# Dense expert blocks written ahead of the last two top-k, and the gate tables' one-hots as contiguous pair blocks

## The chip, the cores and the metric

The kernel runs on one core of one Trainium2 chip. The metric is device time in microseconds (us) of one execution. The engines are named as in the profile: PE is TensorE (matmul; PEld is its weight load, which overlaps), DVE is VectorE, ACT is ScalarE, POOL is GpSimd, SP is SyncE, whose queue issues most of the DMA transfers. PEclk is the TensorE clock that was granted, as a share of full speed.

## The reference

One layer of a decoder is computed for 1056 tokens (1024 prompt, 32 sample), width 1024. It is a mixer (RWKV-7 and pooling, not touched here), then a layer of 16384 single-neuron experts, then an input gate and norms. The change lies in the expert layer:

```
q = (xb @ wq).reshape(128, 8, 2, 128)                  # 8 heads, two halves of the key
s1, s2 = q[:, :, 0] . sub_keys[0], q[:, :, 1] . sub_keys[1]     # 128 scores each
v1, i1 = lax.top_k(s1, 16);  v2, i2 = lax.top_k(s2, 16)
cand = v1[..., :, None] + v2[..., None, :]             # 256 candidates
sc, ci = lax.top_k(cand, 16)
expert = e1 * 128 + e2                                 # e1, e2: i1, i2 at the winners
gate = softmax(sc)
act = gelu(u_tab[expert] . xb) * gate                  # 8 * 16 experts a token
out = sum(act * v_tab[expert])
```

## The kernel before, in words

The program is a list of instructions that a list scheduler has ordered for each engine; where two instructions are ready at once, the one that was written first goes first. Each engine then runs its own list strictly in order. SBUF memory comes from pools that stand on a left and a right stack. A pool that is opened where another was closed takes its memory, and the first writer of a tile waits for the last reader of what lay there.

**Ahead of the experts.** Projections, the RWKV scan in chunks, then for each group of tokens the output projection and the scores. `phase_c` puts the scores of a tile of 128 tokens into DRAM (`scs`, copied by ACT at L750, to `sc_d`), and `top` reads them back in four quarters (`scq`, two buffers, by SP's queue at L759).

**Top-k.** `top` and `select` run for each tile of 128 tokens, nearly all on DVE (L762 to L852, some 120 instructions a tile) with short steps on ACT (copies, the exponential at L830) and POOL (`code`, and half of the `oh` steps at L848).

**Two ways through the experts.** Of the 1056 tokens 672 take the *dense* way, in which all 16384 experts are computed for them as matmuls and multiplied by a table of gates that is zero nearly everywhere. The other 384, three tiles of 128, take the *gather* way: for every token its 8 x 16 rows of `u` and of `v` are fetched by indirect DMAs.

**Gate tables (dense way).** The end of `select` makes them from two one-hots. For four tokens at a time, a tile `ab` holds three blocks of 128 x 4: the one-hot of e1, the one-hot of e2 times the high part of the gate, and times the low part. L875 (DVE) compares an iota with e1 and e2 in one operation of 1024 elements, L877 (DVE) and L878 (POOL; DVE in every third) multiply 512 elements each, and eight matmuls of 128x128 (L881) make the table of four tokens in PSUM. ACT copies it out (L882). `e16` holds e1, e2 and the gates' two parts, each as 128 tokens in a row. There are 168 such steps, from 771 to 1377 us of the span, interleaved with the projections and scores of the later groups.

**Dense blocks.** There are 128 expert blocks of 128. `ublock(b)` loads a block of uT (`eraw`, three buffers, SP's queue, L1060), splits it in a high and a low part (`ehi` on ACT at L1062, `elo` on DVE at L1064, two buffers each), runs 48 matmuls of 336 columns (L1086) and a gelu on ACT (L1092). `ugate(b)` multiplies by the gates (DVE L1148) and splits the product into `wh` (ACT L1150) and `wl` (DVE L1152) in pool `dw`. After each eight blocks (VG = 8) come eight `vblock`s, which load and split a block of vP in the same manner and run 48 matmuls each over the eight `wh`/`wl`. "U8" and "V03" below are ublock 8 and the vblock of group 0, column block 3. The first eight ublocks are run early (`upre`), into tiles `OT0` to `OT7`.

**Order around the change.** The pools `ws`, `mv`, `wc`, `tk` (top-k) stand on one stack of pools, `phases`. Three calls of `top` for the gather tiles come last in it; then `phases` is closed, `dw` and the gather's `rows` are opened on the memory that was freed, and the loop over the dense blocks begins. After it in the text, thus behind it in rank, stand the gather tiles: per row POOL issues an indirect DMA (L1189), DVE does one operation of 1024 elements (L1197 for `u`, L1206 for `v`). Each tile ends with eight transposes on PE (L1216). The layer's last part (`Tail`, input gate and norms, L1234 and on) ends the program.

Of the kernel before, what the change touches and what calls it, by code (L numbers as in the profile page):

```python
# [20 lines left out]
KB = D // 128  # L21
# [40 lines left out]
def body(ctx, tc, io):  # L62
    nc = tc.nc
    mm = nc.tensor.matmul
# [19 lines left out]
    def v3(ap, n):  # L84
        return ap.rearrange("p (a b) -> p a b", b=n)
# [667 lines left out]
    def top(tk, pos, m):  # L753
        V12 = tk.tile([128, HEADS, 2, TOPK], F32, name="V12", bufs=1)
        I12 = tk.tile([128, HEADS, 2, TOPK], U32, name="I12", bufs=1)
        for i in range(16):
            if i % 4 == 0:
                sq = tk.tile([128, 4, 128], F32, name="scq", bufs=2)
                nc.sync.dma_start(sq[:m], sc_d[TIDX[pos], :m, i:i + 4, :])  # L759
            s_ = sq[:m, i % 4, :]  # L760
            v8, i8 = V12[:m, i // 2, i % 2, :], I12[:m, i // 2, i % 2, :]
            nc.vector.max(v8[:, 0:8], s_)  # L762
            nc.vector.max_index(i8[:, 0:8], v8[:, 0:8], s_)  # L763
            s2 = tk.tile([128, 128], F32, name="s2", bufs=2)
            nc.vector.match_replace(s2[:m], v8[:, 0:8], s_, -BIG)  # L765
            nc.vector.max(v8[:, 8:16], s2[:m])
            nc.vector.max_index(i8[:, 8:16], v8[:, 8:16], s2[:m])  # L767
            yield
        yield from select(tk, pos, m, V12, I12)


    def select(tk, col, m, V12, I12):
# [87 lines left out]
        ps = PS("b3")  # L860
        for i in range(3):
            src = e12[:m, i, :] if i < 2 else gl[:m].rearrange("p a b -> p (a b)")
            nc.tensor.transpose(ps[:, i * 128:i * 128 + m], src, ident[:m, :m])
        e16 = gp.tile([128, 4, 128], F16, name="e16")
        pe = v3(ps, 128)
        ACT(e16[:, 0:2, :m], pe[:, 0:2, :m], AF.Copy)
        ACT(e16[:, 2, :m], pe[:, 2, :m], AF.Copy, scale=GS)
        STT(e16[:, 3, :m], pe[:, 2, :m], GS, e16[:, 2, :m], op0=ALU.mult, op1=ALU.subtract)
        for t1 in range(0, m, TC):
            st = gp.tile([128, EB, TC], F32, name="gst", bufs=2)  # L870
            for t2 in range(0, TC, 4):
                ps = PS("b3")
                t = t1 + t2
                ab = gp.tile([128, 3, EB, 4], F16, name="ab", bufs=3)
                TT(ab[:, 0:2], iota16[:, None, :, :].to_broadcast([128, 2, EB, 4]),  # L875
                   e16[:, 0:2, None, t:t + 4].to_broadcast([128, 2, EB, 4]), op=ALU.is_equal)
                TT(ab[:, 2], ab[:, 1], e16[:, 2, None, t:t + 4].to_broadcast([128, EB, 4]), op=ALU.mult)  # L877
                GLO(t)(ab[:, 1], ab[:, 1], e16[:, 3, None, t:t + 4].to_broadcast([128, EB, 4]), op=ALU.mult)  # L878
                for i in range(4):
                    for k in (2, 1):  # L880
                        mm(ps[:, i * 128:(i + 1) * 128], ab[:, k, :, i], ab[:, 0, :, i], start=k == 2, stop=k == 1)  # L881
# [147 lines left out]
                pass  # L1029


    ws = phases.enter_context(tc.tile_pool(name="ws", bufs=2))
    mv = phases.enter_context(tc.tile_pool(name="mv", bufs=1))
    work = phases.enter_context(tc.tile_pool(name="wc", bufs=1))
    tk = phases.enter_context(tc.tile_pool(name="tk", bufs=1))
    gstack = ExitStack()
    gp = gstack.enter_context(tc.tile_pool(name="gp", bufs=1))
    iota16 = gp.tile([128, EB, 4], F16, name="iota16")
    it = gp.tile([128, EB, TC], F32, name="gst", bufs=2)[:, :, 0:4]
    nc.gpsimd.iota(it, pattern=[[1, EB], [0, 4]], base=0, channel_multiplier=0, allow_small_or_imprecise_dtypes=True)  # L1040
# [9 lines left out]
    NWT = 3  # L1050
    DP = ((0, NH), (NH, NH))
    U = {}
    LOW = 0

    def PD():
        return dps.tile([128, 2, 512], F32, name="pd")
# [43 lines left out]
    for step in range(1, NG + 1):  # L1100
# [16 lines left out]
        if step == NG - 1:  # L1117
# [6 lines left out]
                nc.sync.dma_start(XH[:, k, :].bitcast(F32), xh_d[:, k, :])  # L1124
                nc.sync.dma_start(XL[:, k, :].bitcast(F32), xl_d[:, k, :])
            xs = [(XH[:, k, :], XL[:, k, :]) for k in range(KB)]
    for col in range(0, GT, 128):
        with tc.high_priority(offset=LOW if col else 0):
            for _ in top(tk, GB + col, min(128, GT - col)):
                pass  # L1130
    phases.close()

    NROW = 7
    dw = ctx.enter_context(tc.tile_pool(name="dw", bufs=1, reuse_waits="tile"))
    rstack = ExitStack()
    rows = rstack.enter_context(tc.tile_pool(name="rows", bufs=1, reuse_waits="tile"))
    dpt = ctx.enter_context(tc.tile_pool(name="dpt", bufs=2, space=bass.MemoryType.PSUM, reuse_waits="tile"))


    Ws, gqs = {}, {}  # L1140

    def ugate(b):
        if b % GQ == 0:
            gqs[0] = gqp.tile([128, NTC, GQ, TC], F32, name="gq")
            nc.sync.dma_start(gqs[0], g_d[b // GQ])
        wt_ = U[b]
        w3 = wt_.rearrange("p (c t) -> p c t", t=TC)
        TT(w3, w3, gqs[0][:, :, b % GQ, :], op=ALU.mult)  # L1148
        wh = dw.tile([128, ND], F32R, name="wh", bufs=VG + 1)
        ACT(wh, wt_, AF.Copy)  # L1150
        wl = dw.tile([128, ND], F32R, name="wl", bufs=VG + 1)
        TT(wl, wt_, wh.bitcast(F32), op=ALU.subtract)  # L1152
        Ws[b] = (wh, wl)

    def vblock(g, db):
        w = esplit(io["vP"][g, db])
        ps = PD()
        emm(ps, w, [Ws[b] for b in range(g * VG, (g + 1) * VG)], DP)
        if g:
            TT(halves(OT[db]), ps[:, :, :NH], halves(OT[db]), op=ALU.add)  # L1160
        else:
            ACT(halves(OT[db]), ps[:, :, :NH], AF.Copy)
        if g == EB // VG // 2:
            ht = wt_tile()
            nc.sync.dma_start(ht, hT_d[:, db, GA:GB])
            TT(OT[db], OT[db], ht, op=ALU.add)

    for g in range(EB // VG + 1):
        for b in range(g * VG, min((g + 1) * VG, EB)):
            if b not in U:  # L1170
                ublock(b)
            ugate(b)
            if b == g * VG and g:
# [216 lines left out]
```

## Time and profile before

| | |
|---|---|
| median of 3 runs | 3432.76 us (3430.71 to 3433.68) |
| profiled execution | 3432.96 us |
| its span | 3431.3 us |
| PE busy | 3233.8 us, 94% of the span |
| DVE busy | 2675.9 us, 78% |
| POOL busy | 1788.5 us, 52% |
| ACT busy | 1190.1 us, 35% |

The profiled execution is 0.2 us above the median, and 1.7 us of it lie outside the span. One slice of the page's 40 is 85.8 us. From about 1480 us to the end the dense blocks' matmuls run nearly without a gap. In front of them, from 771 to 1377 us, DVE is busy 573.3 of 606 us and PE 560.1. Between the two stages PE stands still once, for 59.7 us.

### The profile page before, as it was taken

The numbers are of one execution on the slowest core, as the hardware profiler recorded it, in microseconds if no ns is written. First come the engines' busy times: TensorE is split into PE (matmuls) and PEld (weight loads), VectorE is DVE, ScalarE is ACT, GpSimd is POOL, SyncE is SP. The second block draws the span as 40 slices with busy tenths as digits, with TensorE's granted clock in tenths as the row PEclk, the third lists the DMA queues.
The fourth block names the chain that finished last, engine by engine and source line by source line (L and its number), as shares of the span: only waits on it lengthen the run. The fifth ranks groups of instructions, "written<-read, shape, count | busy, mean of one in ns | idle before, by whom it ended". The sixth has DMA issues, their size and how long they took to land.

```text
span 3431.3 us, 57620 instructions
## 1 busy us (share of the span) xinstructions
PE 3233.8 (94%) x21831; PEld 3142.4 (92%) x21831; DVE 2675.9 (78%) x5365; ACT 1190.1 (35%) x1776; POOL 1788.5 (52%) x1434
## 2 busy tenths in 40 slices
PE   8997998999999899489999999999999999999997
PEld 7876988999989888489999999999999999999997
DVE  6777333269999889788888888888888888888656
ACT  6452523345555555222212222222222122222343
POOL 5434334235465365256666666665566666666225
PEclk9997999999999999789999999999999999999999
DMA  4567645768767877459999999998989999999524
GB/s 167 206 210 193 176 132 139 217 180 229 195 194 217 267 233 226 168 207 341 335 326 342 334 342 326 340 346 314 342 329 335 329 337 348 326 330 339 173 81 130
DMA packets 467861, 883.61 MB, mean 258 GB/s; under 512 B 129280, under 2 KB 252416, under 8 KB 463104
## 3 DMA queue, kind: packets, MB, share of 16 engines
q1 hardware_dynamic: 356992, 477.24, 43.3%
q0 software_dynamic: 110592, 402.70, 32.0%
q8 instruction: 171, 2.80, 0.3%
q14 instruction: 106, 0.87, 0.1%
HBM read 759.22 MB, written 120.60 MB: 256 GB/s over the span
## 4 chain that ended last, share of the span: by engine, by line
PE 71%; DVE 15%; DMA 4%; POOL 2%; issue 1%; ACT 1%; SPq 0%; DVEq 0%; ACTq 0%; POOLq 0%
PE pd L1086 56%; DVE ab L875 2%; PE ps L881 2%; PE ps L661 2%; PE ps L663 2%; PE ps L662 2%; DVE ab L877 1%; PE ps L526 1%; DMA sraw<-wq 1%; PE ps L521 1%; DVE oh L847 1%; DVE h L718 1%; DVE I L763 1%; DVE s L765 1%; DVE I L767 1%
## 5 line engine op out<-in xcount | busy, mean ns | idle before, releaser
L1189 POOL DMA_INDIRECT row<-v,idx x384 | 533.2, 1389 | 322.8 <-DVE po L1206 147.4
L1189 POOL DMA_INDIRECT row<-u,idx x384 | 538.1, 1401 | 298.8 <-DVE row L1197 119.1
L1062 ACT ACTIVATE ehi<-eraw 128x1024 fp32r<-128x1024 f32 x278 | 294.8, 1060 | 1140.4 <-PE pd L1086 1088.6
L1086 PE MATMUL pd<-wh,ehi 128*128 128x336 f32 (+1 forms) x2112 | 507.1, 319 | 66.2 <-ACT wh L1150 59.7
L1086 PE MATMUL pd<-XH,elo 128*128 128x336 f32 x2176 | 515.5, 318 | 4.5 <-POOL elo L124 2.8
L1086 PE MATMUL pd<-XL,ehi 128*128 128x336 f32 x2176 | 514.8, 317 | 0.0
L1086 PE MATMUL pd<-XH,ehi 128*128 128x336 f32 x2176 | 512.7, 316 | 0.0
L1086 PE MATMUL pd<-wl,ehi 128*128 128x336 f32 (+1 forms) x2112 | 506.9, 319 | 0.7 <-DVE wl L1152 0.7
L1086 PE MATMUL pd<-wh,elo 128*128 128x336 f32 (+1 forms) x2112 | 506.7, 319 | 0.0
L1206 DVE SCALAR_TENSOR_TENSOR po<-row,act,po 128x1024 f32<-128x1024 f32 x381 | 488.1, 1281 | 6.5
L1197 DVE SCALAR_TENSOR_TENSOR row<-row,xt 128x1024 f32<-128x1024 f32 x384 | 455.7, 1219 | 3.9 <-DMA row<-u,idx 3.6
L1086 PEld LDWEIGHTS pd<-wh,ehi 128*128 128x128 f32 x2112 | 363.8, 189 | 67.2 <-ACT wh L1150 59.9
L1064 DVE TENSOR_TENSOR elo<-eraw,ehi 128x1024 fp32r<-128x1024 f32 x256 | 316.8, 1238 | 109.6 <-ACT ehi L1062 103.6
L1086 PEld LDWEIGHTS pd<-XH,elo 128*128 128x128 f32 x2176 | 373.5, 188 | 5.6 <-POOL elo L124 3.4
L1086 PEld LDWEIGHTS pd<-XH,ehi 128*128 128x128 f32 x2176 | 372.6, 189 | 0.3
L1086 PEld LDWEIGHTS pd<-XL,ehi 128*128 128x128 f32 x2176 | 371.3, 188 | 0.2
L1086 PEld LDWEIGHTS pd<-wl,ehi 128*128 128x128 f32 x2112 | 364.3, 188 | 1.1 <-DVE wl L1152 1.1
L1086 PEld LDWEIGHTS pd<-wh,elo 128*128 128x128 f32 x2112 | 364.4, 188 | 0.2
L1160 DVE TENSOR_TENSOR OT<-pd,OT 128x672 f32<-128x672 f32 x120 | 102.8, 857 | 173.7 <-PE pd L1086 173.6
L881 PE MATMUL ps<-ab 128*128 128x128 f16 x1344 | 197.1, 295 | 26.9 <-DVE ab L877 10.7
L124 POOL TENSOR_TENSOR ab<-ab,e 128x512 f16<-128x512 f16 x110 | 127.0, 1157 | 169.2 <-DVE ab L877 134.1
L882 ACT ACTIVATE gst<-ps 128x512 f32<-128x512 f32 x168 | 179.5, 1101 | 99.4 <-PE ps L881 98.6
(505 smaller groups left out, 5966.5 us busy)
## 6 DMA issues: line engine op xcount, KB each, us to landing
eraw<-uT SPq DMA_DIRECT2D x128, 512.0 KB, 6.6
eraw<-vP SPq DMA_DIRECT2D x128, 512.0 KB, 6.8
g_d<-gst SPq DMA_DIRECT2D x21, 2048.0 KB, 8.1
gq<-g_d SPq DMA_DIRECT2D x32, 1344.0 KB, 9.8
whi<-wc_d SPq DMA_DIRECT2D x148, 256.0 KB, 4.2
wlo<-wc_d SPq DMA_DIRECT2D x148, 256.0 KB, 4.6
wc_d<-shi SPq DMA_DIRECT2D x40, 256.0 KB, 2.6
wc_d<-slo SPq DMA_DIRECT2D x40, 256.0 KB, 3.0
```

The lines of the kernel that those rows point to most:

```text
L124: nc.gpsimd.tensor_tensor(out, a, b, op=op)
L661: mm(ps[:, :n], whi[:, kk, :], xhi[:, k, :n], start=k == 0, stop=False)
L662: mm(ps[:, :n], whi[:, kk, :], xlo[:, k, :n], start=False, stop=False)
L881: mm(ps[:, i * 128:(i + 1) * 128], ab[:, k, :, i], ab[:, 0, :, i], start=k == 2, stop=k == 1)
L882: ACT(st[:, :, t2:t2 + 4].rearrange("p e t -> p t e"), v3(ps, 128), AF.Copy, scale=1.0 / GS)
L1062: ACT(hi, raw, AF.Copy)
L1064: sub(lo, raw, hi.bitcast(F32), op=ALU.subtract)
L1086: mm(ps[:, a, :n], w_[:, k, :], x_[:, s:s + n], start=first, stop=last)
L1160: TT(halves(OT[db]), ps[:, :, :NH], halves(OT[db]), op=ALU.add)
L1189: nc.gpsimd.indirect_dma_start(out=r[:m], out_offset=None, in_=io[tab], in_offset=bass.IndirectOffsetOnAxis(ap=idx[:m, hh, k:k + 1], axis=0))
L1197: STT(r[:m], r[:m], 1.0, xt[:m], op0=ALU.mult, op1=ALU.mult, accum_out=pre[:m, k:k + 1])
L1206: STT(po[:m], r[:m], act[:m, k:k + 1], po[:m], op0=ALU.mult, op1=ALU.add)
```

## The change

**Order and memory.** `tk` is opened first, at the bottom of the stack, and keeps track of its memory by tile. `ws`, `mv` and `wc` go into a stack of their own, `cstack`, which is closed after the first gather tile's top-k. `dw` is opened right then on the other side of memory. The loop over the dense blocks becomes a function: its first 18 blocks (0 to 17, with the vblocks of groups 0 and 1) are written ahead of the top-k of the other two gather tiles, the rest behind it. `rows` and the transposes' PSUM pool come after, as before. The offset of 0 in `high_priority` was without effect and goes.

**One-hots.** `ab` has six blocks of 128 x 2 in place of three of 128 x 4: a block belongs to two tokens. The comparison is still one operation of 1024 elements, and the multiplications have 512 each. `e16` holds for every four tokens e1, e2 and the two parts of the gate side by side, 16 values. The operand that repeats along the 128 experts is then a row of two values (4 bytes) instead of four (8 bytes). The matmuls read a token's one-hot at a step of 2 elements instead of 4.

```diff
-        e16 = gp.tile([128, 4, 128], F16, name="e16")
-        ACT(e16[:, 0:2, :m], pe[:, 0:2, :m], AF.Copy)
...
+        e16 = gp.tile([128, 32, 4, 4], F16, name="e16")
+        ej = e16.rearrange("p q j t -> p j q t")[:, :, :nq]
+        ACT(ej[:, 0:2], pe[:, 0:2], AF.Copy)
...
-                ab = gp.tile([128, 3, EB, 4], F16, name="ab", bufs=3)
-                TT(ab[:, 0:2], iota16[:, None, :, :].to_broadcast([128, 2, EB, 4]),
-                   e16[:, 0:2, None, t:t + 4].to_broadcast([128, 2, EB, 4]), op=ALU.is_equal)
-                TT(ab[:, 2], ab[:, 1], e16[:, 2, None, t:t + 4].to_broadcast([128, EB, 4]), op=ALU.mult)
-                GLO(t)(ab[:, 1], ab[:, 1], e16[:, 3, None, t:t + 4].to_broadcast([128, EB, 4]), op=ALU.mult)
+                ab = gp.tile([128, 6, EB, 2], F16, name="ab", bufs=3)
+
+                def pairs(j, n):
+                    e = e16[:, t // 4, j:j + n // 2].rearrange("p j (a b) -> p (j a) b", b=2)
+                    return e[:, :, None, :].to_broadcast([128, n, EB, 2])
+
+                TT(ab[:, 0:4], iota16[:, None, :, :].to_broadcast([128, 4, EB, 2]), pairs(0, 4), op=ALU.is_equal)
+                TT(ab[:, 4:6], ab[:, 2:4], pairs(2, 2), op=ALU.mult)
+                GLO(t)(ab[:, 2:4], ab[:, 2:4], pairs(3, 2), op=ALU.mult)
                 for i in range(4):
-                    for k in (2, 1):
-                        mm(ps[:, i * 128:(i + 1) * 128], ab[:, k, :, i], ab[:, 0, :, i], start=k == 2, stop=k == 1)
+                    for k in (4, 2):
+                        mm(ps[:, i * 128:(i + 1) * 128], ab[:, k + i // 2, :, i % 2], ab[:, i // 2, :, i % 2],
+                           start=k == 4, stop=k == 2)
...
-    ws = phases.enter_context(tc.tile_pool(name="ws", bufs=2))
-    mv = phases.enter_context(tc.tile_pool(name="mv", bufs=1))
-    work = phases.enter_context(tc.tile_pool(name="wc", bufs=1))
-    tk = phases.enter_context(tc.tile_pool(name="tk", bufs=1))
+    tk = phases.enter_context(tc.tile_pool(name="tk", bufs=1, reuse_waits="tile"))
+    cstack = ExitStack()
+    ws = cstack.enter_context(tc.tile_pool(name="ws", bufs=2))
+    mv = cstack.enter_context(tc.tile_pool(name="mv", bufs=1))
+    work = cstack.enter_context(tc.tile_pool(name="wc", bufs=1))
...
-    for col in range(0, GT, 128):
-        with tc.high_priority(offset=LOW if col else 0):
-            for _ in top(tk, GB + col, min(128, GT - col)):
-                pass
-    phases.close()
-
-    NROW = 7
-    dw = ctx.enter_context(tc.tile_pool(name="dw", bufs=1, reuse_waits="tile"))
+    gtop(0)
+    cstack.close()
+    dw = ctx.enter_context(tc.tile_pool(name="dw", bufs=1, side="right", reuse_waits="tile"))
...
-    for g in range(EB // VG + 1):
-        for b in range(g * VG, min((g + 1) * VG, EB)):
...
+    def dense(b0, b1):
+        for b in range(b0, b1):
+            if b < EB:
+                if b not in U:
+                    ublock(b)
+                ugate(b)
+            if b % VG == 0 and b:
                 for db in range(KB):
-                    vblock(g - 1, db)
...
+                    vblock(b // VG - 1, db)
+
+    NB0 = 2 * VG + 2
+    dense(0, NB0)
+    for col in range(128, GT, 128):
+        gtop(col)
+    phases.close()
...
+    dense(NB0, EB + 1)
```

PE, DVE, POOL and SP execute as many instructions as before; ACT has two more table loads. Three places show how the order moves. In the rows the names carry the number of their tile.

ACT, at the end of the scores. Before: behind the copies of the last scores (L750) come the steps of both top-k's, and only then the `wh` of the eight ready ublocks, whose names are `OT0` to `OT7`:

```order
L750 ACTIVATE scs_15211<-ps_15206 128x512
L1062 ACTIVATE ehi_16199<-eraw_16197 128x1024
L1092 ACTIVATE wt_16132<-pd_16077 128x672
L776 ACTIVATE F12_15588<-I12_15483 128x8x16 x2
L830 ACT_TABLE_LOAD
L830 ACTIVATE gt_15708<-gt_15708 128x128
L820 ACTIVATE KI_15700<-K16_15667 128x128
L824 ACTIVATE cF_15704<-ci_15702 128x128
L776 ACTIVATE F12_15856<-I12_15751 128x8x16 x2
L1150 ACTIVATE wh_16036<-OT0_14002 128x672
L1150 ACTIVATE wh_16041<-OT1_14122 128x672
```

Now (L1152 is the old L1150, L1164 the copy of a vblock's result, L1069 the old L1062):

```order
L750 ACTIVATE scs_15211<-ps_15206 128x512
L1152 ACTIVATE wh_15491<-OT0_14002 128x672
...
L1152 ACTIVATE wh_15528<-OT7_15132 128x672
L1069 ACTIVATE ehi_15654<-eraw_15652 128x1024
L1099 ACTIVATE wt_15587<-pd_15532 128x672
L1152 ACTIVATE wh_15592<-wt_15587 128x672
L1069 ACTIVATE ehi_15710<-eraw_15708 128x1024
L1164 ACTIVATE OT0_14002<-pd_15602 128x672
L776 ACTIVATE F12_17160<-I12_17055 128x8x16 x2
```

The eight `wh` moved from behind the second top-k's `F12` to right behind the scores, and the top-k's steps now stand among the splits and copies of the vblocks.

DVE, same place. Before, the `wl` of the same eight tiles stand between rows of the last tile's second top-k, some 200 rows behind the wait for `scq_15562`, which is the last quarter of scores of the second gather tile:

```order
L1064 TENSOR_TENSOR elo_16201<-eraw_16197,ehi_16199 128x1024
L1148 TENSOR_TENSOR wt_16132<-wt_16132,gq_16134 128x672
L762 MAX V12_15482<-scq_15562 128x8 x4
...
L805 MATCH_REPLACE s2_15908<-SC_15876,cand_15859 128x50
L1152 TENSOR_TENSOR wl_16038<-OT0_14002,wh_16036 128x672
L805 MATCH_REPLACE s2_15915<-SC_15876,cand_15859 128x50
```

Now:

```order
L767 MAX_INDEX I12_17055<-V12_17054,s2_17130 128x8
L1154 TENSOR_TENSOR wl_15493<-OT0_14002,wh_15491 128x672
...
L1154 TENSOR_TENSOR wl_15530<-OT7_15132,wh_15528 128x672
L1071 TENSOR_TENSOR elo_15656<-eraw_15652,ehi_15654 128x1024
L1150 TENSOR_TENSOR wt_15587<-wt_15587,gq_15589 128x672
L762 MAX V12_17054<-scq_17134 128x8 x4
```

All eight `wl` stand ahead of the wait for that quarter (`scq_17134`). Behind it the 243 instructions of the two top-k's stand in runs between the `elo` of V02 to V07 and U9 to U15: some 18 ahead of that of V02, then 13 to some 40 from one `elo` to the next. The first row operation of the gather (old L1197) comes at place 2700 of DVE's list, where it was 2683.

PE, end of the gather: the eight transposes of the third tile's result (`po_32407`). Before, inside a ublock:

```order
L1086 MATMUL pd_29947<-XL_13152,ehi_29950 128x336 x2
L1216 MATMUL pt_33210<-ident_77,po_32407 128x128 x4
L1216 MATMUL pt_33216<-ident_77,po_32407 128x128 x4
L1086 MATMUL pd_29947<-XH_13151,elo_29952 128x336 x2
L1086 MATMUL pd_29947<-XH_13151,ehi_29950 128x336 x2
```

Now, inside a vblock that comes 433 matmuls later in PE's list (place 20831 in place of 20398):

```order
L1093 MATMUL pd_30495<-wh_30067,elo_30493 128x336
L1229 MATMUL pt_33210<-ident_77,po_32407 128x128 x4
L1229 MATMUL pt_33216<-ident_77,po_32407 128x128 x4
L1093 MATMUL pd_30495<-wh_30067,elo_30493 128x336
L1093 MATMUL pd_30495<-wh_30131,ehi_30491 128x336 x2
```

The other tiles' transposes move by 427 and 442 places; the sequence of the blocks on PE is the same (V00 and V01, whose first matmuls alternated, now stand one behind the other). The first vblock's matmuls begin at place 9176 in both. The matmul that needs the last tile's result, the sum for a norm at L1234 (new L1247), stands at place 21154 in both, and the tail's work on the gather tiles begins at place 21443.

More of the change, by code (lines that the diff above doesn't have):

```diff
@@ L863, in select @@
             nc.tensor.transpose(ps[:, i * 128:i * 128 + m], src, ident[:m, :m])
-        e16 = gp.tile([128, 4, 128], F16, name="e16")
-        pe = v3(ps, 128)
-        ACT(e16[:, 0:2, :m], pe[:, 0:2, :m], AF.Copy)
-        ACT(e16[:, 2, :m], pe[:, 2, :m], AF.Copy, scale=GS)
-        STT(e16[:, 3, :m], pe[:, 2, :m], GS, e16[:, 2, :m], op0=ALU.mult, op1=ALU.subtract)
+        nq = m // 4
+        e16 = gp.tile([128, 32, 4, 4], F16, name="e16")
+        ej = e16.rearrange("p q j t -> p j q t")[:, :, :nq]
+        pe = v3(ps, 128)[:, :, :m].rearrange("p j (q t) -> p j q t", t=4)
+        ACT(ej[:, 0:2], pe[:, 0:2], AF.Copy)
+        ACT(ej[:, 2], pe[:, 2], AF.Copy, scale=GS)
+        STT(ej[:, 3], pe[:, 2], GS, ej[:, 2], op0=ALU.mult, op1=ALU.subtract)
         for t1 in range(0, m, TC):
@@ L1029, in body @@
                 pass
-    ws = phases.enter_context(tc.tile_pool(name="ws", bufs=2))
-    mv = phases.enter_context(tc.tile_pool(name="mv", bufs=1))
-    work = phases.enter_context(tc.tile_pool(name="wc", bufs=1))
-    tk = phases.enter_context(tc.tile_pool(name="tk", bufs=1))
+    tk = phases.enter_context(tc.tile_pool(name="tk", bufs=1, reuse_waits="tile"))
[3 more added lines that the diff above has]
+    work = cstack.enter_context(tc.tile_pool(name="wc", bufs=1))
     gstack = ExitStack()
     gp = gstack.enter_context(tc.tile_pool(name="gp", bufs=1))
-    iota16 = gp.tile([128, EB, 4], F16, name="iota16")
-    it = gp.tile([128, EB, TC], F32, name="gst", bufs=2)[:, :, 0:4]
-    nc.gpsimd.iota(it, pattern=[[1, EB], [0, 4]], base=0, channel_multiplier=0, allow_small_or_imprecise_dtypes=True)
+    iota16 = gp.tile([128, EB, 2], F16, name="iota16")
+    it = gp.tile([128, EB, TC], F32, name="gst", bufs=2)[:, :, 0:2]
+    nc.gpsimd.iota(it, pattern=[[1, EB], [0, 2]], base=0, channel_multiplier=0, allow_small_or_imprecise_dtypes=True)
     nc.vector.tensor_copy(iota16, it)
@@ L1052, in body @@
     U = {}
-    LOW = 0
     def PD():
@@ L1126, in body, with gtop @@
             xs = [(XH[:, k, :], XL[:, k, :]) for k in range(KB)]
-    for col in range(0, GT, 128):
-        with tc.high_priority(offset=LOW if col else 0):
-            for _ in top(tk, GB + col, min(128, GT - col)):
-                pass
-    phases.close()
-    NROW = 7
-    dw = ctx.enter_context(tc.tile_pool(name="dw", bufs=1, reuse_waits="tile"))
-    rstack = ExitStack()
-    rows = rstack.enter_context(tc.tile_pool(name="rows", bufs=1, reuse_waits="tile"))
-    dpt = ctx.enter_context(tc.tile_pool(name="dpt", bufs=2, space=bass.MemoryType.PSUM, reuse_waits="tile"))
+    def gtop(col):
+        for _ in top(tk, GB + col, min(128, GT - col)):
+            pass
+    gtop(0)
+    cstack.close()
+    dw = ctx.enter_context(tc.tile_pool(name="dw", bufs=1, side="right", reuse_waits="tile"))
     Ws, gqs = {}, {}
@@ L1166, in vblock @@
             TT(OT[db], OT[db], ht, op=ALU.add)
-    for g in range(EB // VG + 1):
-        for b in range(g * VG, min((g + 1) * VG, EB)):
[L1170 to L1173, printed above, removed]
-                for db in range(KB):
-                    vblock(g - 1, db)
-        if g == EB // VG:
-            for db in range(KB):
-                vblock(g - 1, db)
+    def dense(b0, b1):
[5 more added lines that the diff above has]
+            if b % VG == 0 and b:
+                for db in range(KB):
+                    vblock(b // VG - 1, db)
[4 more added lines that the diff above has]
+    phases.close()
+    NROW = 7
+    rstack = ExitStack()
+    rows = rstack.enter_context(tc.tile_pool(name="rows", bufs=1, reuse_waits="tile"))
+    dpt = ctx.enter_context(tc.tile_pool(name="dpt", bufs=2, space=bass.MemoryType.PSUM, reuse_waits="tile"))
+    dense(NB0, EB + 1)
     for col in range(0, GT, 128):
```

## The prediction

> **What bounds the kernel now.** I read the page's slices first. PE is full from slice 18 to the end, and one slice in the middle is not.
>
> ```profile
> span 3431.3 us, 57620 instructions
> PE   8997998999999899489999999999999999999997
> DVE  6777333269999889788888888888888888888656
> PEclk9997999999999999789999999999999999999999
> ```
>
> Slice 16 (from 1373 us) shows PE at 4 and the clock at 7: PE stands still there. The waits of PE name the reason, and the timeline has both ends of it.
>
> ```profile
> PE pd L1086 <- ACT wh L1150: 59.7, 1, 59.7
> 1411.16 0.46 PE L1086 MATMUL pd<-XH,elo 128*128 128x336 f32 x2
> 1471.29 1.49 PE L1086 MATMUL pd<-wh,ehi 128*128 128x336 f32 x4 [59.67 <-ACT wh L1150]
> 1473.46 0.93 PE L1086 MATMUL pd<-wl,ehi 128*128 128x336 f32 x2 [0.68 <-DVE wl L1152]
> 1470.47 5.35 ACT L1150 ACTIVATE wh<-OT 128x672 fp32r<-128x672 f32 x8 [2.94 <-POOL code L124]
> ```
>
> U8 ends at 1411.6, and V00 needs `wh`, which ACT makes only at 1470.5. ACT waited for POOL's `code`, a step of the last top-k. The stages around it read thus (busy us of PE, PEld, DVE, ACT, POOL; then PEclk, DMA share, GB/s):
>
> ```profile
> 771.00:1377.00 606.00, 560.14 (x4448) 532.35 (x4447) 573.29 (x2195) 331.76 (x511) 321.87 (x314) 0.96 0.74 222
> 1411.30:1501.20 89.90, 29.55 (x174) 28.85 (x173) 79.00 (x460) 17.09 (x28) 17.37 (x33) 0.66 0.12 37
> 1600.00:2000.00 400.00, 400.00 (x2592) 400.00 (x2591) 345.10 (x408) 91.86 (x108) 256.44 (x183) 1.00 0.92 332
> ```
>
> So the one-hot stage is bound by DVE (573 of 606 us), the top-k's between the stages by DVE, and everything behind by PE, one matmul each 400/2592 = 0.1543 us. A block of 48 takes 7.41 us. What PE gets earlier at 1411 it keeps to the end, if nothing else becomes late.
>
> **Part 1: the eight `wh` and `wl` ahead of the top-k.** Three things must be there for V00: the gated tiles, ACT, and the vP block.
>
> ```profile
> 1393.10 8.43 DVE L1148 TENSOR_TENSOR OT<-OT,gq 128x672 f32<-128x672 f32 x8 [15.09 <-DMA gq<-g_d]
> 1408.28 0.60 ACT L750 ACTIVATE scs<-ps 128x512 f32<-128x512 f32 x1 [0.30 <-PE ps L747]
> 1418.80 0.87 DVE L762 MAX8 V<-scq 128x8 f32<-128x128 f32 x4 [4.36 <-DMA scq<-sc_d]
> ```
>
> The gates are in by 1401.5. The new memory of `wh` holds nothing that is read later: its first writer waits, beside the gates, for two loads of `wlo` from the scores' stage. ACT's list has `wh` right behind the last scores, so the first starts at 1408.9 and is done at 1409.6 (5.35/8 = 0.67 us each). V00's own split is ahead of that in the lists. DVE has its eight `wl` ahead of the quarter that arrives at 1418.8, so they fall into time in which it waited. V00 uses one `wh`/`wl` pair each 0.93 us, and ACT and DVE make one in 0.67 and 0.85. V00 starts at U8's end: the waits of 59.67 and 0.68 go, **−60.4 us**.
>
> With the stop goes the slow clock behind it:
>
> ```profile
> 1470.00:1475.00 5.00, 3.03 (x9) 2.60 (x10) 5.00 (x36) 4.53 (x7) 0.44 (x1) 0.50 0.02 5
> 1475.00:1480.00 5.00, 5.00 (x26) 5.00 (x26) 5.00 (x18) 1.48 (x3) 0.00 (x0) 0.75 0.00 0
> 1480.00:1485.00 5.00, 5.00 (x34) 5.00 (x33) 4.99 (x35) 1.00 (x2) 0.00 (x0) 1.00 0.00 0
> ```
>
> From the first matmul (1471.3, less the 0.68 counted above) to 1477.5 a pair takes about 0.56 us instead of 0.31: some 10 pairs, **−2.4 us**.
>
> **Part 2: the two top-k's among the blocks.** They are DVE work that nothing covered, and now dense work runs beside them. How much is it? DVE was busy 79.0 us from 1411.3 to the first gather at 1501.2. Of that the same window has 5.70 in four `elo` and 7.47 + 0.85 in `wl` and the gates, so 65.0 is top-k.
>
> ```profile
> 1411.30:1501.20 89.90, 5.70 (x4) 0.66 0.12 37
> 1411.30:1501.20 89.90, 7.47 (x9) 0.66 0.12 37
> 1411.30:1501.20 89.90, 0.85 (x1) 0.66 0.12 37
> L1064 DVE TENSOR_TENSOR elo<-eraw,ehi 128x1024 fp32r<-128x1024 f32 x256 | 316.8, 1238 | 109.6 <-ACT ehi L1062 103.6 <-PE pt L1234 5.2
> 1501.19 1.15 POOL L1189 DMA_INDIRECT row<-u,idx  x1 [1.70 <-DVE gl L850]
> ```
>
> By the order the top-k's are spread up to U13 or U14. To U13, PE has 13 blocks (V00 to V07, U9 to U13), 13 x 7.41 = 96.3 us. DVE has 65.0 of top-k, 8 `wl` (6.7), 12 `elo` at 1.24 (14.9) and five pairs of gate and `wl` at 1.7 (8.5), 95.1 us. The two are level on the sum, but the runs are uneven: up to some 40 instructions at 65.0/243 = 0.27 us stand between two `elo`, 10.7 us against a block's 7.41. The `elo` have two buffers, so DVE can be one block ahead and no more. In addition SP's queue, which loads the vP and uT blocks, now has the quarters of scores between them, which wait for DVE's use of two `scq` buffers; and ACT, which makes `ehi`, waits in between for the top-k's results. I put in **+6 us** of stalls: the lower end is 0 (DVE one block ahead throughout), the upper 22. That is the case where four of the runs are that long and each stops PE for 10.7 + 1.24 − 7.41 = 4.5 us, and the wait for a quarter of scores seen at 1418.8, 4.4 us, is felt too. I am nearer to the lower end since the sum is level and the short runs ahead of V06 and V07 give room.
>
> **Part 3: the gather starts later.** DVE comes to the first row at about 1411 + 95 + 6 = 1512 us, 11 later than at 1501. The rows end at PE place 20831 in the new order, 433 later. PE would be there at 1411.6 + (20831 − 9176) x 0.1543 + 6 = 3216, and before it was there at
>
> ```profile
> 3207.84 0.87 PE pt L1216 x8
> 3208.71 107.95 PE pd L1086 x700
> 3221.62 10.40 POOL L124 TENSOR_TENSOR rg<-rg,tg 128x384 f32<-128x384 f32 x7 [29.14 <-ACT tg L1228]
> ```
>
> The rows' own pace: they ended just ahead of 3208 and now start 11 later, so they end at about 3215 to 3219 if they keep it. DVE is 86% busy in the long stage (345 of 400) and POOL 64%, so there is some room to catch up. I put in **+1 us** for the third transposes, between 0 and 11. Behind them, the matmul that needs the result stands at place 21154, 323 matmuls or 50 us later, and the way to it (store, load, squares, and POOL's sum of them to 3232.0) took 24 us before; the 433 places are paid out of that cover. Were it gone, PE would wait there.
>
> **Part 4: the one-hots.** Same counts of instructions and elements on DVE and POOL.
>
> ```profile
> L878 DVE TENSOR_TENSOR ab<-ab,e 128x512 f16<-128x512 f16 x58 | 33.0, 568 | 0.2
> 1424.63 1.28 ACT L830 ACT_TABLE_LOAD   x1
> L875 DVE TENSOR_TENSOR ab<-iota,e x168: 655/682/2704, 771.5 to 1367.5; 128x1024 f16<-128x1024 f16 x168
> L877 DVE TENSOR_TENSOR ab<-ab,e x168: 384/412/2327, 779.4 to 1370.2; 128x512 f16<-128x512 f16 x168
> L834 DVE TENSOR_TENSOR gt<-gt,sm x9: 266/274/292, 746.6 to 1484.3; 128x128 f32<-128x128 f32 x8, 32x128 f32<-32x128 f32 x1
> L881 PEld LDWEIGHTS <-ab x1344: 111/117/257, 780.1 to 1376.7; 128*128 128x128 f16 x192
> L519 PEld LDWEIGHTS <-id x81: 96/98/152, 334.6 to 1138.9; 128*128 128x128 f16 x80, 64*64 64x64 f16 x1
> ```
>
> L875 does 512 elements more than L877 in 0.27 us, so two elements in 1.05 ns, and 0.14 us is the fixed part. L834 has 128 elements of 4 bytes, with one word of `sm` repeated 16 times; 128 x 1.05 ns + 0.14 us is 0.274, just its median. A repeated word is thus read at the pace of a stream, and the new row of two 16-bit values is one such word. I take no change on DVE (0). The lower end is also 0, since two results in 1.05 ns is the best pace of these rows. The upper end is one result in 1.05 ns, priced below. A matmul's weight load took 0.117 us at the step of 8 bytes and 0.098 where the weights lie side by side (L519). At 4 bytes it may be between: 1344 x 0.019 = 26 us of PE at most. But DVE sets the pace there, so I take **−2 us**, between −20 and 0 (a loss has no reason, since the step gets smaller). ACT's copies into the finer `e16` are a few in a stage in which it is 55% busy, and its two table loads (1.28 us each, as L830's) lie in part 2's range.
>
> **The sum.** 3433.0 (the profiled execution, 0.2 above the median) − 60.4 − 2.4 + 6 + 1 − 2 = **3375 us**, 1.7% faster. What a measurement can tell from no change is about 0.2%, 7 us.
>
> **The rivals.**
>
> *Slower: the one-hots lose their pace (0.07).* If a row of one word, read 128 times, makes DVE fall back to one element at a time, L875 grows by 512 x 1.05 ns = 0.54 us and L877, and the 58 of L878 on DVE, by 0.27. That is 168 x 0.54 + 226 x 0.27 = 152 us in a stage where DVE has 33 us idle, so about +119, and 3375 + 119 = 3494. It decides once the growth is above 58 + 33 = 91 us of DVE. L834 speaks against it; no operation before has such rows with f16.
>
> *About the same: they lose a part of it (0.07).* The pairs stay, but each step from word to word costs some more. At half the growth, 76 us, less the 33 idle, the time is 3418; at two thirds, 101 us, it is 3443. [...]
>
> *Smaller gain: the stretch stays bound by DVE (0.16).* The stalls of part 2 come to 20 to 45 us since waits of DVE for POOL's `oh` and `code` come on top of the 95 us, and each wait passes to PE. The time would be 3390 to 3415. For it: DVE and PE are level there. Against it: in the same steps before, DVE was idle only 10.9 us of 89.9.
>
> *Given back at the end (0.05).* The rows end 30 us or more behind the PE place of the third transposes. PE stops there, and the time is about 3405.
>
> *More gain: PE's weight loads (0.05).* If the stage is paced by PE too, 15 to 26 us come off: 3350 to 3360.
>
> *The forecast (0.60)*: 3360 to 3390.
>
> The numbers follow. The range 3352 to 3405 holds the forecast, two thirds of the smaller gain, the give-back and most of the fourth, 0.60 + 0.11 + 0.05 + 0.04 = 0.80. Faster: 0.60 + 0.16 + 0.05 + 0.05 and 0.02 of the partial loss, 0.88. Same: 0.03 of the partial loss. Slower: the full loss 0.07 and 0.02 of the partial one, 0.09.
>
> **What would show it.** Right: PE has no wait of 59.7 us on `wh`; the first `wh` from an `OT` starts at about 1409; slices 16 and 17 show PE at 9 and the clock near 10; the first indirect DMA comes at 1506 to 1520; the waits of PE on `ehi` or `elo` from 1411 to 1515 sum to under 15 us; the comparison (new L882 or next to it) still has a median of 0.68 us; the third tile's transposes run at about 3215 without a wait. Wrong: a one-hot stage that ends later than 1377, with the comparison at 1.0 us or more; PE waits of over 25 us on DVE up to 1520; or a PE wait at the third transposes or the norm's matmul at place 21154.

## The result and the profile after

The changed kernel takes 3352.99 us (median of 4 runs, 3346.63 to 3355.36) where the kernel before took 3431.74 beside it. The ratio is 0.9767, with an interval of 0.9750 to 0.9784. Two repeats, told of below, gave 0.9780 (0.9765 to 0.9796) and 0.9782 (0.9767 to 0.9796). It is faster by 2.2 to 2.3%, 75 to 79 us; 58 were forecast. The profiled execution of 3346.63 us is the fastest of all, and a part of its gain is its own luck, as the repeats show.

The head of the page and its slices, as they were shown of before:

```profile
span 3344.9 us, 57622 instructions
PE   8997999998888888999999999999999999999997
DVE  6777332359999989889888888888889888888966
PEclk9998999999999989999999999999999999999998
```

The hole of slice 16 is gone. In its place the slices 9 to 15 of PE, the one-hots, went from 9 to 8 (one was at 8 before): PE has less to do there, and the stage is hardly shorter. The timeline at the old hole, ACT and then PE, with the first indirect DMA and the only wait of PE up to 1520 us:

```profile
1393.23 0.60 ACT L750 ACTIVATE scs<-ps 128x512 f32<-128x512 f32 x1 [0.29 <-PE ps L747]
1393.72 5.34 ACT L1152 ACTIVATE wh<-OT 128x672 fp32r<-128x672 f32 x8
...
1396.11 0.47 PE L1093 MATMUL pd<-XH,elo 128*128 128x336 f32 x2
1396.42 0.47 PE L1093 MATMUL pd<-wh,ehi 128*128 128x336 f32 x2
...
1493.42 1.50 POOL L1202 DMA_INDIRECT row<-u,idx  x1 [1.71 <-DVE gl L850]
...
1509.90 0.85 PE L1093 MATMUL pd<-XH,elo 128*128 128x336 f32 x2 [2.06 <-DVE elo L1071]
```

`wh` starts as the last scores' copy ends, and V00 follows U8 without a gap. The stretch of the two top-k's, from V00 to the first gather, and the stage of the one-hots, in the columns of before (PE, PEld, DVE, ACT, POOL, clock, DMA share, GB/s):

```profile
1396.40:1493.40 97.00, 97.00 (x633) 96.75 (x632) 92.66 (x474) 35.26 (x49) 20.29 (x32) 1.00 0.27 94
771.00:1377.00 606.00, 518.48 (x4516) 481.70 (x4515) 563.67 (x2186) 331.31 (x514) 333.37 (x316) 0.95 0.76 228
1600.00:2000.00 400.00, 400.00 (x2607) 400.00 (x2606) 351.75 (x419) 100.27 (x120) 259.87 (x185) 1.00 0.93 339
```

In the first row PE is busy all 97.0 us and DVE 92.7 beside it. The last row has a surprise: 2607 matmuls in 400 us, where there were 2592. The one-hots' own lines, with that of PE's matmuls before (L881) on top:

```profile
L881 PE MATMUL ps<-ab 128*128 128x128 f16 x1344 | 197.1, 295 | 26.9 <-DVE ab L877 10.7 <-ACT gst L882 4.8 <-DVE ab L878 4.5
L882 DVE TENSOR_TENSOR ab<-iota,e x168: 660/686/2337, 765.9 to 1353.7; 128x1024 f16<-128x1024 f16 x168
L883 DVE TENSOR_TENSOR ab<-ab,e x168: 390/416/2293, 772.8 to 1356.5; 128x512 f16<-128x512 f16 x168
L887 PEld LDWEIGHTS <-ab x1344: 96/97/258, 774.9 to 1362.2; 128*128 128x128 f16 x192
L887 PE MATMUL ps<-ab 128*128 128x128 f16 x1344 | 126.0, 227 | 60.8 <-DVE ab L883 28.5 <-DVE ab L884 10.8 <-POOL ab L124 9.9
```

DVE's comparison takes 0.686 us where it took 0.682, so the row of one word keeps its pace. PE's weight load takes 0.097 us instead of 0.117 and its matmuls are busy 126.0 us instead of 197.1, but PE now stands idle ahead of them for 60.8 us instead of 26.9. Of that 49.2 us (28.5, 10.8 and 9.9) are waits for `ab`, where it was 19.1.

The difference of the two spans, 86.4 us, splits at three rows of the timeline. U8's end, put here where the next matmul could have started, went from 1411.5 to 1396.4 (15.1). The stop behind it went from 59.8 to 0. The way from V00's first matmul to the norm's matmul at place 21154 went from 1853.4 to 1842.1 (11.3). The tail behind that is 106.6 and 106.4. The second is the predicted one. The first and the third are to be explained.

### The profile page after: what moved, and what is told of

The parts are those of the page before. It is cut to its first block, busy times and chain, and to the rows that moved or that the text cites. A ratio compares the mean times of both kernels' runs of the same rounds, so it can differ in the third digit from the quotient of the medians.

```text
span 3344.9 us, 57622 instructions
## 1 busy us (share of the span) xinstructions
PE 3163.4 (95%) x21831; PEld 3063.6 (92%) x21831; DVE 2661.9 (80%) x5365; ACT 1187.9 (36%) x1778; POOL 1803.7 (54%) x1434
## 4 chain that ended last, share of the span: by engine, by line
PE 69%; DVE 16%; DMA 4%; POOL 2%; issue 2%; ACT 1%; SPq 0%; DVEq 0%; ACTq 0%; POOLq 0%
PE pd L1093 57%; DVE ab L882 3%; DVE ab L883 2%; PE ps L663 1%; PE ps L661 1%; PE ps L662 1%; PE ps L526 1%; DMA sraw<-wq 1%; PE ps L521 1%; DVE oh L847 1%; DVE h L718 1%; DVE I L763 1%; DVE s L765 1%; DVE ab L884 1%; DVE I L767 1%
## 5 line engine op out<-in xcount | busy, mean ns | idle before, releaser
L1202 POOL DMA_INDIRECT row<-v,idx x384 | 543.4, 1415 | 314.2 <-DVE po L1219 142.6
L1069 ACT ACTIVATE ehi<-eraw 128x1024 fp32r<-128x1024 f32 x278 | 295.0, 1061 | 1098.3 <-PE pd L1093 955.2
L661 PE MATMUL ps<-hi,whi 128*128 128x256 f32 (+1 forms) x592 | 180.0, 305 | 12.0 <-DMA whi<-wc_d 7.4
```

What stands on the lines that cost most here:

```text
L661: mm(ps[:, :n], whi[:, kk, :], xhi[:, k, :n], start=k == 0, stop=False)
L1069: ACT(hi, raw, AF.Copy)
L1202: nc.gpsimd.indirect_dma_start(out=r[:m], out_offset=None, in_=io[tab], in_offset=bass.IndirectOffsetOnAxis(ap=idx[:m, hh, k:k + 1], axis=0))
```

## Experiments: which part of the change

**The one-hots alone, the order alone, and the whole again.** The first is the kernel before with the change's hunk in `select` and the new `iota16`; the second is the changed kernel with the old ones; the third and a later one are the changed kernel as it is.

> The kernel before with the new one-hots and nothing else. Theory A: the new one-hots shorten the stage because PE's weight loads and matmuls on them get shorter (their median 0.117 to about 0.097 and 0.297 to about 0.218 us), although DVE's three operations keep 0.68, 0.41 and 0.41 us; U8 ends 8 to 15 us earlier than at 1411.6 and the time is 3417 to 3425. Theory B: the 15 us by which U8 ended earlier in the changed kernel come from elsewhere (the pools' new places or the spread of the runs); then this is 3428 to 3434, and U8 ends within 4 us of 1411.6. In both the stop of 60 us on wh stays, and the vblocks' matmuls keep their 154.9 ns.

> The changed kernel with the old one-hots: only the order and the pools are new. Theory A: U8 ends 8 to 15 us later than in the changed kernel (1396.4), so 3361 to 3369. Theory B: U8 ends where it does in the changed kernel, 3350 to 3357. In both the stop on wh is gone, stalls up to the first gather are 0 to 5 us, and by theory C (below, at the third run) the vblocks' matmuls take 153.2 ns each.

> The changed kernel once more, for its spread and a second trace. Theory C: the vblocks' matmuls take 153.2 ns each, where they took 154.9 before, because wh and wl lie elsewhere in SBUF; this trace shows 153.0 to 153.4 again. Theory D: the 1.7 ns are a matter of the single run; this trace shows 154 or more in them when its time is nearer to the others' 3353. Expected time 3350 to 3357.

> The changed kernel a third time. Its first profiled execution had U8's end at 1396.4, its second at 1410.2; ten others with the same work ahead of it lie from 1401 to 1413. If the first is the end of a spread, U8 ends at 1405 to 1412 here and the median of the time is 3354 to 3363; if the two values are two states, this one is within 3 us of the one or the other.

| kernel | median us (runs) | ratio to before | U8's end | V00's start | place 21154 | span |
|---|---|---|---|---|---|---|
| before, its profile | 3432.76 (3) | | 1411.5 | 1471.3 | 3324.7 | 3431.3 |
| changed, first | 3352.99 (4) | 0.9767 (0.9750 to 0.9784) | 1396.4 | 1396.4 | 3238.5 | 3344.9 |
| one-hots alone | 3428.93 (11) | 0.9984 (0.9973 to 0.9994) | 1409.5 | 1468.5 | 3322.2 | 3429.8 |
| order alone | 3363.43 (5) | 0.9789 (0.9776 to 0.9803) | 1413.2 | 1413.2 | 3256.0 | 3362.5 |
| changed, again | 3362.77 (5) | 0.9780 (0.9765 to 0.9796) | 1410.2 | 1410.2 | 3254.4 | 3361.1 |
| changed, third | 3359.37 (5) | 0.9782 (0.9767 to 0.9796) | 1409.2 | 1409.2 | 3251.2 | 3357.7 |

The order and the pools make nearly all of the gain. The one-hots make 0.16% alone, 5 us with an interval of 2 to 9, and inside the change nothing that these runs can tell from zero (3362.77 against 3363.43 on one chip). Their waits show where a part of PE's saving went, here in the kernel with the one-hots alone:

```profile
PE pd L1093 <- ACT wh L1157: 58.8, 1, 58.8
PE ps L887 <- DVE ab L883: 28.4, 31, 3.0
PE ps L887 <- DVE ab L884: 9.7, 17, 1.4
```

PE's work shrank by some 70 us and its wait on DVE's `ab` (10.7 and 4.5 before) grew. Theory A, in which 8 to 15 us come from them, falls: the order alone is inside its range of time, but the changed kernel itself, run beside it, came to the same time. Theory B holds for the one-hots alone. Its time for the order alone (3350 to 3357) was missed, and so was the 3350 to 3357 expected of the first repeat, since both were reckoned from the first measurement. U8's end at 1396.4 was the end of a spread: of the profiled runs of all kernels with the products shared as here, five with the old one-hots ended U8 between 1406.9 and 1413.2 and eight others with the new ones between 1406.6 and 1410.2. Their means are 1411.4 and 1408.9. Why that one run was some 13 us quicker than the two repeats ahead of U8 is open. More than half of it cannot come from the one-hots: the first comparison (L882) already starts at 765.9 us there, and at 773.1 and 773.6 in the repeats.

**The top-k written first again, with the new pools.**

```diff
-    NB0 = 2 * VG + 2
+    NB0 = 0
```

> The changed kernel with its pools, but with the two last top-k written ahead of all dense blocks, as before. By the prediction's part 1 what freed wh was the order as much as the memory. Theory E (the memory alone): the order that comes out is nearly the same, wh runs right behind the last scores, no stop of 60 us, and the time is that of the changed kernel, 3357 to 3366. Theory F (the text's order is needed, since DVE does the top-k first): PE stops for its elo, 20 to 50 us in all, 3380 to 3410.

3361.48 us, ratio 0.9790 (0.9772 to 0.9809). Theory E: it is the changed kernel's time. ACT's rows are the same too:

```profile
1406.92 0.60 ACT L750 ACTIVATE scs<-ps 128x512 f32<-128x512 f32 x1 [0.30 <-PE ps L747]
1407.41 5.34 ACT L1152 ACTIVATE wh<-OT 128x672 fp32r<-128x672 f32 x8
```

In the list that the scheduler makes of it, the order on PE, ACT, POOL and SP is the same, and on DVE only two `elo` and one `wl` stand 5 to 7 places later. So with the new pools "dense blocks ahead of the top-k" in the text does nothing. The pools do. The built program gives the addresses. In the kernel before `wh` and `wl` lie from 20992 to 69375 and the tiles of `tk` only from 74080 on, so it was not these that `wh` waited for. The first `wh` lies on `iotaC` (20992 to 21191), a constant that POOL's step `code` of every top-k reads, and that is the wait of the row `[2.94 <-POOL code]` in the prediction. The change leaves `iotaC` there and opens `dw` at 58208. No run moves `iotaC` alone, so that it alone made the stop is argued from these addresses and that row, not shown.

**Only `dw` on the other side.** The kernel before with `side="right"` for `dw`, without moving `tk`.

> The kernel before with only the pool of wh and wl opened on the other side of memory, where the change puts it; the gather's rows then lie where wh and wl were. Its stop on wh gets longer, since wh now stands behind more of ACT's list (behind a gelu of the gather's first rows): some 40 to 70 us more, 3460 to 3500. What counts is the pace of the vblocks' matmuls in the long stage: theory C expects 153.0 to 153.4 ns, theory D 154.5 to 155.

3460.84 us in one run, and the stop is longer:

```profile
PE pd L1086 <- ACT wh L1150: 93.0, 1, 93.0
```

`dw` there lies on addresses 58208 to 106591 and `tk` still from 74080 on. The first `wh` is free of `iotaC`, but the second (79712) lies on tiles of `tk`, and in ACT's list all of them stand behind a step of the gather's first rows. So moving `dw` alone is not enough. Moving `tk` alone was not tried.

## Experiments: why the vblocks got quicker

From one matmul's start to the next, between 1620 and 2600 us (some 3000 matmuls of each kind, steps above 0.2 us left out), a matmul of a vblock takes 155.30 ns before and 153.34 after, one of a ublock 153.87 and 153.47. (The expectations give such figures 0.1 to 0.5 ns lower, in all kernels: they were counted over windows of 50 us, and matmuls at a window's edge were counted twice.) For a reader of the timeline: the first matmul of a group of eight vblocks (384 matmuls) and the first of the ublocks behind, before and after:

```profile
2186.86 0.32 PE L1086 MATMUL pd<-wh,ehi 128*128 128x336 f32 x1
2246.31 0.32 PE L1086 MATMUL pd<-XH,ehi 128*128 128x336 f32 x1
```

```profile
2108.74 0.47 PE L1093 MATMUL pd<-wh,ehi 128*128 128x336 f32 x2
2167.62 0.32 PE L1093 MATMUL pd<-XH,ehi 128*128 128x336 f32 x1
```

59.45 us became 58.88. The group shown is one of the quicker ones before; the others but the first, behind the stop, took 59.4 to 60.2. The operands and the count are the same; what moved is the memory. `wh` and `wl` start at 20992 (a multiple of 128 bytes) before and at 58208 (96 beyond one) after; the weights `ehi` and `elo` start 96 beyond a multiple of 128 in both. Each experiment moves something by a few bytes with an unused tile, as here, or with 32 bytes (`[128, 8]`). In the kernel before the tile also moves the gather's rows, which start at 0 in the changed kernel and at 96 in the one with 96 bytes:

```diff
     dw = ctx.enter_context(tc.tile_pool(name="dw", ...))
+    dw.tile([128, 24], F32, name="dpad")
```

> The kernel before with 32 bytes left free ahead of wh and wl, so that each of their rows, and the gather's tiles behind them, starts 32 bytes later; the instructions and their order are the same. The vblocks' matmuls took 155.1 ns with wh and wl where the kernel before has them and 153.2 to 153.4 in every run that has them elsewhere. Theory C1 (the start of a row within 64 bytes matters: before at a multiple of 64, in the changed kernel 32 beyond one, like the operand of the ublocks): 153.0 to 153.5 ns here, and about 10 us off the time, 3421 to 3425. Theory C2 (the region of SBUF matters): 155 ns here too, 3430 to 3436.

> The kernel before with 96 bytes left free ahead of wh and wl. At 32 bytes the vblocks' matmuls went from 155.0 to 154.05 ns, half of the way. Theory C1a (the place within 128 bytes counts, and 96, where the changed kernel has wh and wl, is the quick one): 152.9 to 153.4 ns, and 8 to 14 us off the time. Theory C1b (a half of it is the place within 64 bytes, the other half the region): 154.0 ns as at 32 bytes, 5 to 9 us off.

> The changed kernel with wh and wl 96 bytes earlier, so that their rows start at multiples of 128 bytes, in the same region. Theory C1: the vblocks' matmuls take 154.7 to 155.2 ns, the time grows by about 10 us against the changed kernel (3362.8 on this chip), 3370 to 3375. Theory C2: 153.2 ns and 3358 to 3365.

> The changed kernel with wh and wl 32 bytes earlier, 64 beyond a multiple of 128. With 96 beyond the vblocks' matmuls take 153.1 ns, with 0 beyond 155.2. Theory C1a (quick only at 96): 154 to 155.2 ns. Theory C1c (slow only at 0): 153.0 to 153.4 ns.

> The changed kernel with everything that the blocks' matmuls read 32 bytes earlier: wh, wl, XH, XL (streamed) and ehi, elo (loaded as weights) all start 64 bytes beyond a multiple of 128, where they started 96 beyond. With wh and wl alone at 64 the vblocks' matmuls took 155.4 ns. Theory K (what counts is where the streamed operand starts): both kinds of blocks take 155.0 to 155.6 ns, about 13 us more than the changed kernel in a comparable run, and more in the ublocks. Theory L (what counts is that streamed operand and weights start at the same place): 153.0 to 153.5 ns in both.

> The same with ehi and elo left at 96 beyond: only the streamed operands wh, wl, XH and XL start at 64. Theory K: 155.0 to 155.6 ns in both kinds of blocks. Theory L: the same here. A third theory M (the vblocks alone are sensitive, for a reason of their own) expects 153.0 to 153.5 ns in the ublocks and 155.0 to 155.6 in the vblocks, in this run and in the other.

| kernel | wh, wl beyond a multiple of 128 | XH, XL | weights | vblock ns | ublock ns | time us |
|---|---|---|---|---|---|---|
| before | 0 | 96 | 96 | 155.30 | 153.87 | |
| before, 32 later | 32 | 96 | 96 | 154.24 | 153.35 | ratio 0.9978 (0.9966 to 0.9989) |
| before, 96 later | 96 | 96 | 96 | 153.34 | 153.75 | ratio 0.9974 (0.9965 to 0.9984) |
| before, `dw` on the right | 96 | 96 | 96 | 153.40 | 153.76 | 3460.84 (one run), the longer stop |
| changed | 96 | 96 | 96 | 153.34 | 153.47 | 3352.99; repeats 3362.77, 3359.37 |
| changed, 96 earlier | 0 | 96 | 96 | 155.36 | 153.70 | 3373.2, ratio 0.9831 (0.9812 to 0.9849) |
| changed, 32 earlier | 64 | 96 | 96 | 155.63 | 153.36 | 3370.67 (one run) |
| changed, all 32 earlier | 64 | 64 | 64 | 153.34 | 153.49 | 3362.31 (one run) |
| changed, streamed 32 earlier | 64 | 64 | 96 | 155.84 | 154.45 | 3374.03 (one run) |

Theory D is out, since the repeats have 153.3 ns too. The region of memory (theory C2) is out: at 96 the low region is as quick as the high one (153.34 ns in both), and at 0 the high one as slow as the low (155.36 and 155.30). C1b falls at 96, where it expected 154.0, and C1 and C1c fall at 32 and at 64, where the pace is not the quick one (154.24 and 155.63). The last two rows settle most of the rest; these two kernels differ in the place of `ehi` and `elo` alone. With everything at 64 both kinds of blocks have their full pace (153.34 and 153.49 ns), and with the weights alone left at 96 both lose (155.84 and 154.45). So among the places tried it is not the place of the streamed operand that counts but its place against the weights' within 128 bytes (theory L). Theories K and M fall on the vblocks of the first run. The ublocks of the second lost less than theory L expected of them (155.0 to 155.6). The group of vblocks in these two kernels, first all moved, then the streamed ones:

```profile
2122.03 0.32 PE L1097 MATMUL pd<-wh,ehi 128*128 128x336 f32 x1
2180.91 0.32 PE L1097 MATMUL pd<-XH,ehi 128*128 128x336 f32 x1
```

```profile
2123.77 0.32 PE L1097 MATMUL pd<-wh,ehi 128*128 128x336 f32 x1
2183.67 0.32 PE L1097 MATMUL pd<-XH,ehi 128*128 128x336 f32 x1
2242.99 0.32 PE L1097 MATMUL pd<-wh,ehi 128*128 128x336 f32 x1
```

58.88 against 59.90 us, and 59.32 for the ublocks between. Over the program's 6144 matmuls of the vblocks, 1.7 ns (155.13 to 153.43 over their whole stretch) make 10.4 us, most of the 11.3. Why the ublocks differ by some tenths of a ns where nothing of theirs moved, and why 32 costs half of what 0 and 64 cost, is open. The second halves of the streamed rows start 64 bytes off the first (336 columns are 1344 bytes), so one offset stands for two, and also in the quick kernels only the first halves start at the weights' place.

## Experiments: what bounds the one-hots' stage

```diff
     def GLO(t):
-        return PTT if t % 12 else TT
+        return PTT                      # all on POOL; all on DVE: TT; every second on DVE: t % 8
```

> The changed kernel with all 168 products with the gates' low part on POOL (58 of them were on DVE, 33 to 35 us of DVE; POOL gets 58 x 1.2 = 70 us more, with some 270 us idle in the stage). Theory G: the stage is bound by DVE, which is why 71 us of PE saved by the new one-hots bought next to nothing; then U8 ends 15 to 30 us earlier than at 1410, and the time is 3335 to 3350. Theory H: it is bound by the chain through POOL and PE of each step; then nothing or a loss, 3360 to 3385.

> The changed kernel with all 168 products with the gates' low part on DVE and none on POOL. With all on POOL the stage got 30 us longer, and DVE's own operations beside them slower (the product with the high part 0.69 us on the mean instead of 0.57, its median alone 0.42). Theory I (POOL's operation holds DVE's up, so one on POOL costs DVE nearly what it costs there): DVE has 110 x 0.42 = 46 us more and gets back up to 168 x (0.15 + 0.19) = 57 us, and the stage ends 5 to 25 us earlier: 3335 to 3358. Theory J (the time on POOL is mostly free for DVE): 10 to 40 us longer, 3370 to 3400.

> The changed kernel with every second of these products on DVE (84) instead of every third (58). Theory I: 3350 to 3360, between the changed kernel and all on DVE. Theory J: 3365 to 3375.

All on POOL: 3393.44 us, ratio 0.9884 (0.9866 to 0.9902), U8's end 1440.4. All on DVE: 3356.46, 0.9780 (0.9767 to 0.9794), U8's end 1401.4. Every second: 3361.33, 0.9794 (0.9779 to 0.9809). The groups of the first and then of the second of these kernels:

```profile
L124 POOL TENSOR_TENSOR ab<-ab,e 128x512 f16<-128x512 f16 x168 | 199.3, 1193 | 147.8 <-DVE ab L883 106.5 <-PE ps L662 8.5 <-PE ps L663 4.8
L882 DVE TENSOR_TENSOR ab<-iota,e 128x1024 f16<-128x1024 f16 x168 | 151.6, 909 | 12.5 <-PE ps L887 7.5 <-ACT e L868 5.0
L883 DVE TENSOR_TENSOR ab<-ab,e 128x512 f16<-128x512 f16 x168 | 115.0, 693 | 0.8
```

```profile
L882 DVE TENSOR_TENSOR ab<-iota,e 128x1024 f16<-128x1024 f16 x168 | 124.5, 750 | 7.0 <-PE ps L887 6.7
L884 DVE TENSOR_TENSOR ab<-ab,e 128x512 f16<-128x512 f16 x168 | 84.3, 512 | 0.2
L883 DVE TENSOR_TENSOR ab<-ab,e 128x512 f16<-128x512 f16 x168 | 81.7, 498 | 0.1
```

Theory G falls: with 58 products fewer on DVE the stage got 30 us longer. Theory H has the direction, but the time lies above its 3360 to 3385. DVE's groups on `ab` sum to 266.6 us with none of the low products on DVE and to 290.5 with all 168, so a product on POOL spares DVE 0.14 us, not the 0.42 of its median: DVE's other two operations get longer beside POOL (0.693 against 0.498 us, 0.909 against 0.750). PE waits 23.2 us for POOL's `ab` with all of them on POOL and 10.7 in the first repeat of the changed kernel, and its granted clock from 771 to 1410 us is 0.91 against 0.95. How the rest of the 30 us divides was not tried. With all on DVE the time, 3356.46, is inside theory I's range (3335 to 3358) and far from J's, but no gain is shown: the ratio is 0.9780 as in the first repeat, and U8's end of 1401.4 lies between the changed kernel's own 1396.4 and 1409.2. Every second on DVE lies just above I's 3350 to 3360. No version tried beats the changed kernel, and what bounds the stage stays open.

## Why the prediction was right or wrong, step by step

- **What bounds the kernel, and part 1.** Right. The stop of 59.7 and 0.7 us went whole, `wh` follows the scores, and V00 follows U8. The reason was half right: the memory made `wh` late, but with the new pools the order of the text has no part in it (the run with the top-k written first).
- **The slow clock.** The 2.4 us behind the stop went, but in the first profile a smaller one came: after the 2.06 us wait at 1509.9 the matmuls run at 0.57 of the clock from 1510 to 1514 us (below), at a cost of about 1.5.
- **Part 2, stalls of 6 us.** About the size: 2.06 us in the first profile, and in the first repeat none up to 1520 but four waits of 4.3 us in all from 1521 to 1549. DVE and PE were level, as the sum had it (92.7 of 97.0 us; 95.1 of 96.3 worked out), and the uneven runs cost little. The rivals with stalls of 20 us or more and with a stop at the end did not come.
- **Part 3, the transposes.** Right: PE has no wait there, 0 for 1 us put in. The gather starts 97 us behind V00 (101 worked out). The moments given as signs, 1409 for the first `wh`, 1506 to 1520 for the first indirect DMA and 3215 for the third transposes, came at 1407.5, 1507.1 and 3204.1 in the first repeat; the last is early by the pace told of below. In the first profile they came at 1393.7, 1493.4 and 3188.2, with U8's early end.
- **Part 4, the one-hots.** DVE's pace is kept (0.686 us for the comparison's 1024 elements, 0.682 before), so both rivals on it are out. What L834 showed for a repeated word of 4 bytes (0.274 us for 128 elements) held here for a row of two f16 values. The −2 us stood for what is measured as 2 to 9 alone and nothing measurable inside the change. The reason that it is small was right in this, that PE does not set the pace there: with the one-hots alone its idle time ahead of these matmuls grew from 26.9 to 57.8 us.
- **The step that failed** is a term that the sum does not have. It took PE's pace in the long stage, 400/2592 = 0.1543 us a matmul, as given, and so put the new place of `wh` and `wl` at nothing beyond what waits for that memory. The pace became 400/2607 = 0.1534. Between V00 and the norm's matmul the vblocks went from 155.13 to 153.43 ns, 10.4 us over 6144 matmuls, and the ublocks from 153.77 to 153.51, 1.5 us over some 5800. The slow clock and the stalls there (4.0 us before, 4.6 after) about cancel, which leaves the 11.3. The first repeat's profile (3362.83 us) lies 12 us below the forecast, and 11 of them are the pace; the rest is stalls and one-hots, less than the runs can settle. The first profile (3346.63) lies 28 below, of which 12 are the pace and 13 are U8's early end, which the repeats do not show. The fourth rival (more gain, 3350 to 3360) has the size of the result, but its mechanism, PE's weight loads in the one-hots' stage, is not where it came from: that its range was met is luck.
- **The first measurement** lies 6 to 10 us below the two repeats (3352.99; 3362.77, 3359.37). The ratio says the same with less spread: 0.9767, 0.9780, 0.9782, where the forecast was 0.983. So the forecast of 3360 to 3390 was missed by the first measurement met by the first repeat and missed by 0.6 us by the second, with a gain in both that the sum did not know.

The wait and the clock behind it in the changed kernel, from 1510 to 1514 us (PE's clock is the number before the DMA share):

```profile
1510.00:1514.00 4.00, 4.00 (x16) 4.00 (x17) 4.00 (x8) 2.21 (x3) 3.39 (x3) 0.57 1.02 404
```

## What to carry to other kernels

Where a scheduler orders the program, look first at which memory a late instruction waits for: here the first `wh` lay on a small constant that the top-k reads, the seven others stood behind it in ACT's list, and moving pools did what the text's order had no part in. When a change moves tiles that PE reads, ask where they start against the weights: here their place within 128 bytes made 1.1% of the vblocks' pace (155.13 against 153.43 ns a matmul), 10.4 us, more than any wait that was left of PE in the long stage. Before trusting a gain on one engine, see who waits for it: 70 us less on PE, in a stage in which PE waits for the others, bought at most 9.

## What the runs showed of the hardware that was not expected

- A 336-column matmul of a vblock took 153.3 to 153.4 ns when the streamed tiles and the weights started at the same place within 128 bytes (96 and 96, or 64 and 64), and 154.2 to 155.8 when they did not. In the ublocks it was 153.4 to 153.9 against 154.5.
- Reading f16 one-hots at a step of 4 bytes instead of 8 took PE's weight load from 0.117 to 0.097 us and the matmuls' busy time from 197.1 to 126.0 us for the same 1344 (127.2 with the one-hots alone, 196.9 with the order alone).
- A slow clock followed some of PE's stops of about 2 us and not others. After one of 2.06 us (changed, first, at 1509.9) the granted clock was 0.57 over the next 4 us, and 0.57 also after one of 1.83 us (changed, 32 earlier, at 1543.9). But after stops of 2.21 us (changed, third, at 1522.6) and 2.37 us (changed, all 32 earlier, at 1523.6) it stayed at 1.00.
